# Seven-product matmuls in both MLPs' down projections and both attentions' output projections, with accumulator banks paired by use

## The chip, the cores and the metric

One core of a Trainium2 chip runs the whole program. The metric is the device time of one execution in microseconds. An execution's own time is the span from its first to its last instruction and a little more around it (1.75 us in the profiled one). The engines are TensorE (PE, with its weight loads listed apart as PEld), VectorE (DVE), ScalarE (ACT), GpSimd (POOL) and SyncE (SP). SP issues the transfers of the weights; POOL issues most other transfers.

## What is computed

Two decoder layers on 256 tokens of width 2048, all in fp32. Each layer is a token mixer, a cross-attention to 256 memory rows, and an MLP with a squared ReLU. Layer 0 mixes by a gMLP, layer 1 by an S5 state-space layer.

```python
def memory_attention(h, mem_n, w_q, w_kv, w_o):
    ...
    p = jax.nn.softmax(scores, axis=-1).astype(v.dtype)
    o = jnp.einsum('bhsm,bmhd->bshd', p, v).reshape(bsz, seq, X_HEADS * X_HEAD_DIM)
    return o @ w_o

def squared_relu_mlp(h, w_up, w_down):
    return jnp.square(jax.nn.relu(h @ w_up)) @ w_down
```

`w_o` is 2048 x 2048, `w_up` 2048 x 8192 and `w_down` 8192 x 2048. The change concerns the two products `o @ w_o` and `(...) @ w_down`, in both layers.

## The kernel before

**Precision.** An fp32 product is made of three products of rounded parts: hi x hi, hi x lo and lo x hi. Activations are kept as such pairs. Each weight tile (two row blocks of 128, 512 columns: 128x1024 numbers, 512 KB) is loaded by SP into `wraw` (`wload`, 4 buffers); ACT casts it to `whi` (L101), and DVE subtracts to get `wlo` (L102); `whi` and `wlo` have 3 buffers each. This pair of instructions is called a split below. A tile then feeds 12 matmuls of 128x512: 2 row blocks, 2 halves of the tokens, 3 products. Every weight tile ends with a `tick`.

**A down or output product.** The output is taken in four column blocks `n` of 512. For each, 8 weight tiles are added up in one accumulator (`psA`: 2 accumulators of two banks, one bank for each half of the tokens), and DVE gathers the result into the residual `x`. `w_o` goes through `gemm_tok` (gather at L527), layer 0's `w_down` through `gemm_hid` (matmuls L700 to L702, gather L560). The MLP runs in four quarters of the hidden width: an up stage (`gemm_feat`, 32 tiles of `f_w_up`), then a down stage (4 column blocks, 32 tiles of `f_w_down`).

**The seven-product form.** Layer 1's down products go through `gemm_seven` (seven calls of it; the last two column blocks of the last quarter are done otherwise). A call makes two column blocks at once. Of each block's 8 weight tiles the first two (token halves x row tiles x column blocks: 2 x 2 x 2 blocks) are multiplied in Strassen's manner by 7 block products of 6 matmuls each, instead of 8. The other 12 tiles are direct. The block products need sums of token blocks (`token_sums`, once for each quarter: four operations of 128x256 and one split) and sums of raw weight tiles (L653, L663, L669, L674: 128x1024 each). The raw tiles are fetched into `ws`. Some block results belong to two outputs, so ACT copies them out of the bank (`keep`, L646), and DVE gathers the copies.

**What sets the order.** The program is scheduled when it is built: each engine then runs its instructions in that fixed order and waits in place. SP's loads too are one queue in order. `self.side` holds work that is put between the ticks. In layer 0's MLP this is the preparation of the S5 layer's matrices (`ssm_prep`, L911 to L962): 109 pieces, one every two ticks, each with small operations on DVE, some on PE and ACT, and POOL transfers (`bcq` in, `Qd`, `Kd` and `Pd` out). S5 reads those back as `pq`, `dq` and `qq` (L986). `self.at` puts work a given number of ticks ahead: `nxt.chunk(x, n)` makes column block `n` of the next stage's normalized, transposed activations, with PE transposes (L214). The activations live in the `act` pool, 2 buffers of 128 x 16 x 512 numbers: `hT`, the input of the stage, and in the attention `oT`. Between attention 0 and layer 0's MLP `regroup` (L1235) writes `x` to DRAM and reads it back in another order of rows, 2 MB out and 2 MB in, on POOL's queue.

Of the kernel before, what the change touches and what calls it, by code (L numbers as in the profile page):

```python
# [21 lines left out]
NCH = D // NB  # L22
# [16 lines left out]
class Trunk:  # L39
# [395 lines left out]
    def attention(self, x, layer, cur, nxt):  # L435
# [3 lines left out]
        with tc.tile_pool(name="at", bufs=2, reuse_waits="tile") as ap:  # L439
# [59 lines left out]
            for hd in range(HEADS):  # L499
# [3 lines left out]
                for t in range(2):  # L503
# [19 lines left out]
            nxt.start()  # L523
            for j in range(NCH):
                acc = self.gemm_tok(oT, wo, j)
                xc = x[:, :, j * NB:(j + 1) * NB]
                nc.vector.tensor_tensor(out=xc, in0=acc, in1=xc, op=ALU.add)  # L527
                self.at(1, lambda j=j: nxt.chunk(x, j))


    def mlp(self, x, layer, cur, nxt):
# [3 lines left out]
        with tc.tile_pool(name="ml", bufs=4, reuse_waits="tile") as mp:  # L535
            r2 = mp.tile([P, 32 if layer else 56], F32, name="r2", bufs=1)[:, 0:2]
            for b in range(DFF // D):
                hid = []
                for n in range(NCH):
# [3 lines left out]
                    for i in range(2):  # L543
                        r = mp.tile([P, 2, S], F32, name="r", bufs=2)
# [32 lines left out]

    def token_sums(self, pool, a1, a2):


        v = self.nc.vector
        s = pool.tile([P, 4, 2, P], F32, name="s", tag="ws", bufs=4)
        a11, a21, a12, a22 = (a[:, :, t * P:(t + 1) * P] for a in (a1, a2) for t in range(2))
# [3 lines left out]
        v.tensor_tensor(out=s[:, 3], in0=a12, in1=s[:, 1], op=ALU.subtract)  # L587
        sh = pool.tile([P, 4, 2, P], F32R, name="sh", bufs=1)
        sl = pool.tile([P, 4, 2, P], F32R, name="sl", bufs=1)
        self.split(sh, sl, s)  # L590
        return sh, sl

    def gemm_seven(self, pool, hid, sums, w, n0, k0, gather):

# [39 lines left out]

        plain = {j: list(range(2, KT // KB)) for j in range(2)}

        def direct(j):
            kc = plain[j].pop(0)
            hi, lo = self.wtile(w, n0 + j, kc0 + kc)
            for t in (1, 0):  # L640
                into((t, j), range(KB), lambda kk: token(KB * kc + kk, t), hi, lo, not plain[j])
            self.tick()

        def keep(key):
            t = pool.tile([P, NB], F32, name="kept", bufs=4)
            nc.scalar.copy(out=t, in_=banks[key])  # L646
# [5 lines left out]
        run = pool.tile([P, KB * NB], F32, name="run", bufs=1)  # L652
# [4 lines left out]
        acc0 = self.psA.tile([P, 2, NB], F32, name="acc")  # L657
        banks.update({(t, 0): acc0[:, t, :] for t in range(2)})
# [18 lines left out]
        v.tensor_tensor(out=u3, in0=u3, in1=m5, op=ALU.add)
# [659 lines left out]
```

## Time and profile before

| | |
|---|---|
| Median of 3 runs | 2847.34 us (2844.35 to 2847.85) |
| Profiled execution, its own time | 2847.75 us |
| Its span | 2846.0 us |
| Mean granted TensorE clock | 0.998 |
| HBM read, written | 553.88 MB, 22.94 MB |
| Weight queue (hardware) | 511.77 MB, 58.7% of 16 engines |
| POOL's queue (software) | 65.19 MB, 8.5% |

The stages that matter here, in us from the span's start: attention 0 ends near 674; layer 0's MLP follows until 1424, with down stages at 766 to 858, 954 to 1046, 1144 to 1236 and 1332 to 1424; then S5, attention 1, and layer 1's MLP at the end. Busy times of engines are sums of the records' durations. An idle engine is given with the instruction that released it. The records of PE overlap, so PE's pace is read from the starts.

### The profile page before, as it was taken

The numbers are of one execution on the slowest core, as the hardware profiler recorded it, in microseconds if no ns is written. First come the engines' busy times: TensorE is split into PE (matmuls) and PEld (weight loads), VectorE is DVE, ScalarE is ACT, GpSimd is POOL, SyncE is SP. The second block draws the span as 40 slices with busy tenths as digits, with TensorE's granted clock in tenths as the row PEclk, the third lists the DMA queues.
The fourth block names the chain that finished last, engine by engine and source line by source line (L and its number), as shares of the span: only waits on it lengthen the run. The fifth ranks groups of instructions, "written<-read, shape, count | busy, mean of one in ns | idle before, by whom it ended". The sixth has DMA issues, their size and how long they took to land.

```text
span 2846.0 us, 39638 instructions
## 1 busy us (share of the span) xinstructions
PE 2806.7 (99%) x15196; PEld 2350.1 (83%) x15196; DVE 1913.3 (67%) x2645; ACT 1373.7 (48%) x1767; POOL 204.7 (7%) x380
## 2 busy tenths in 40 slices
PE   8999999999999999999999999999999999999998
PEld 6888888888888888888777788888888888888886
DVE  6765655585778888787577666555556766667665
ACT  5445544444544444444455445444454545445453
POOL 1000000000022222222011000000000000000000
PEclk9999999999999999999999999999999999999999
DMA  8766665567677777777879776565566566565755
GB/s 287 216 208 200 193 181 176 169 178 238 187 221 220 221 220 214 220 224 207 234 243 297 215 211 206 170 182 179 178 185 216 168 215 184 171 215 163 221 156 156
DMA packets 180463, 579.56 MB, mean 204 GB/s; under 512 B 37440, under 2 KB 39664, under 8 KB 179504
## 3 DMA queue, kind: packets, MB, share of 16 engines
q1 hardware_dynamic: 141440, 511.77, 58.7%
q0 software_dynamic: 38688, 65.19, 8.5%
q8 instruction: 119, 1.95, 0.3%
q14 instruction: 72, 0.59, 0.1%
q10 hardware_dynamic: 144, 0.07, 0.0%
HBM read 553.88 MB, written 22.94 MB: 203 GB/s over the span
## 4 chain that ended last, share of the span: by engine, by line
PE 90%; DMA 4%; DVE 3%; ACT 1%; issue 1%; POOL 0%; SPq 0%; DVEq 0%; ACTq 0%; POOLq 0%
PE acc L163 24%; PE acc L165 12%; PE acc L623 9%; PE acc L147 9%; PE acc L146 9%; PE acc L145 9%; PE acc L702 4%; PE acc L701 4%; PE acc L700 4%; DVE wlo L102 1%; PE ps L515 1%; PE ps L459 1%; DMA wraw<-in_f_w_down 1%; ACT whi L101 1%; PE ps L214 1%
## 5 line engine op out<-in xcount | busy, mean ns | idle before, releaser
L102 DVE TENSOR_TENSOR wlo<-wraw,whi 128x1024 fp32r<-128x1024 f32 x924 | 1128.9, 1223 | 721.0 <-ACT whi L101 717.7
L101 ACT CAST whi<-wraw 128x1024 fp32r<-128x1024 f32 x924 | 971.5, 1052 | 1176.5 <-PE acc L163 384.7
L163 PE MATMUL acc<-act,whi 128*128 128x512 f32 x3072 | 1083.6, 396 | 0.6 <-ACT whi L101 0.6
L165 PE MATMUL acc<-act,wlo 128*128 128x256 f32 x3072 | 864.9, 282 | 1.9 <-DVE wlo L102 1.9
L163 PEld LDWEIGHTS acc<-act,whi 128*128 128x128 f32 x3072 | 576.1, 188 | 134.4 <-issue 1.6
L165 PEld LDWEIGHTS acc<-act,wlo 128*128 128x128 f32 x3072 | 580.4, 189 | 6.8 <-DVE wlo L102 3.4
L145 PE MATMUL acc<-whi,act 128*128 128x512 f32 x1248 | 490.7, 393 | 9.5 <-ACT whi L101 8.0
L146 PE MATMUL acc<-wlo,act 128*128 128x512 f32 x1248 | 488.7, 392 | 3.9 <-DVE wlo L102 3.7
L147 PE MATMUL acc<-whi,act 128*128 128x512 f32 x1248 | 487.7, 391 | 0.3 <-DVE act L102 0.3
L145 PEld LDWEIGHTS acc<-whi,act 128*128 128x128 f32 x1248 | 235.2, 188 | 58.9 <-ACT whi L101 8.5
L146 PEld LDWEIGHTS acc<-wlo,act 128*128 128x128 f32 x1248 | 235.2, 188 | 53.5 <-DVE wlo L102 6.3
L147 PEld LDWEIGHTS acc<-whi,act 128*128 128x128 f32 x1248 | 235.3, 189 | 48.5 <-DVE act L102 0.7
L701 PE MATMUL acc<-wlo,hh 128*128 128x512 f32 x544 | 215.2, 396 | 1.2 <-DVE wlo L102 1.2
L700 PE MATMUL acc<-whi,hh 128*128 128x512 f32 x544 | 214.7, 395 | 0.0
L702 PE MATMUL acc<-whi,hl 128*128 128x512 f32 x544 | 214.4, 394 | 0.0
L623 PE MATMUL acc<-whi,hh 128*128 128x512 f32 x378 | 148.1, 392 | 3.4 <-ACT kept L646 2.7
L623 PE MATMUL acc<-wlo,hh 128*128 128x512 f32 x378 | 147.5, 390 | 0.6 <-DVE wlo L102 0.6
L623 PE MATMUL acc<-whi,hl 128*128 128x512 f32 x378 | 147.2, 389 | 0.0
L701 PEld LDWEIGHTS acc<-wlo,hh 128*128 128x128 f32 x544 | 102.2, 188 | 25.2 <-DVE wlo L102 2.5
L702 PEld LDWEIGHTS acc<-whi,hl 128*128 128x128 f32 x544 | 102.2, 188 | 22.7 <-issue 1.6
L700 PEld LDWEIGHTS acc<-whi,hh 128*128 128x128 f32 x544 | 102.2, 188 | 22.7 <-ACT whi L101 0.4
L623 PEld LDWEIGHTS acc<-whi,hh 128*128 128x128 f32 x378 | 70.9, 188 | 21.6 <-ACT kept L646 5.3
(315 smaller groups left out, 2286.3 us busy)
## 6 DMA issues: line engine op xcount, KB each, us to landing
wraw<-in_f_w_up SPq DMA_DIRECT2D x256, 512.0 KB, 4.2
wraw<-in_f_w_down SPq DMA_DIRECT2D x228, 512.0 KB, 4.2
wraw<-in_a_w_in SPq DMA_DIRECT2D x64, 512.0 KB, 4.4
wraw<-in_x_w_q SPq DMA_DIRECT2D x64, 512.0 KB, 3.7
wraw<-in_x_w_k SPq DMA_DIRECT2D x64, 512.0 KB, 3.7
wraw<-in_x_w_v SPq DMA_DIRECT2D x64, 512.0 KB, 3.6
wraw<-in_x_w_o SPq DMA_DIRECT2D x64, 512.0 KB, 3.7
wraw<-in_b_w_out SPq DMA_DIRECT2D x64, 512.0 KB, 4.4
```

The lines of the kernel that those rows point to most:

```text
L101: self.nc.scalar.copy(out=hi, in_=src)
L102: self.nc.vector.tensor_tensor(out=lo, in0=src, in1=hi.bitcast(F32), op=ALU.subtract)
L145: nc.tensor.matmul(out[t], ah[:, kt, sl], hi[:, kk, :], start=st, stop=False)
L146: nc.tensor.matmul(out[t], ah[:, kt, sl], lo[:, kk, :], start=False, stop=False)
L147: nc.tensor.matmul(out[t], al[:, kt, sl], hi[:, kk, :], start=False, stop=en)
L163: nc.tensor.matmul(acc[:, f, :], hi[:, kk, sl], both[:, kt].rearrange("p a s -> p (a s)"), start=st, stop=False, skip_group_check=True)
L165: nc.tensor.matmul(acc[:, f, 0:S], lo[:, kk, sl], ah[:, kt, :], start=False, stop=en, skip_group_check=True)
L214: nc.tensor.transpose(pt[:, kk, t * P:(t + 1) * P], src[:, t, c:c + P], self.ident)
L623: mm = lambda s, m, e: nc.tensor.matmul(out, s, m, start=key not in begun, stop=e, skip_group_check=True)
L700: nc.tensor.matmul(acc[:, t, :], ah[:, kt % 4, sl], hi[:, kk, :], start=st, stop=False)
L701: nc.tensor.matmul(acc[:, t, :], ah[:, kt % 4, sl], lo[:, kk, :], start=False, stop=False)
L702: nc.tensor.matmul(acc[:, t, :], al[:, kt % 4, sl], hi[:, kk, :], start=False, stop=en)
```

## The change

`gemm_seven` now also does layer 0's down products (two calls in each quarter, eight in all) and both output projections (two calls each). Twelve calls are new, and layer 1's MLP keeps its seven. Inside `gemm_seven` the two accumulators are now paired as they become free: `acc[0]` holds the outputs (1,0) and (0,1), `acc[1]` holds (0,0) and (1,1) (token half, column block). All four raw tiles are fetched at the start of a call. The last direct tiles of the two column blocks are interleaved, so that `acc[0]` is complete first, is gathered, and then `acc[1]`.

Room for the buffers: in the attentions, tags that the softmax no longer needs; in layer 0's MLP one tile `room` of 128 x 8 x 1024 numbers in the `act` pool, in the memory that `oT` of attention 0 had. The chunks of the next norm now come in twos behind each call.

```diff
@@ attention
+                if hd == 0:
+                    for fp in range(2):
+                        o = ap.tile([P, 2, S], F32, name="o", tag="e")
+                        nc.scalar.copy(out=o, in_=ops[fp])
+                        ops[fp] = o
+                    sums = self.token_sums(ap.tile([P, KB * NB], F32, name="s", tag="qh"),
+                                           lambda: ap.tile([P, 4, 2, P], F32R, name="sums", tag="kh"), *ops)
...
-            for j in range(NCH):
-                acc = self.gemm_tok(oT, wo, j)
-                xc = x[:, :, j * NB:(j + 1) * NB]
-                nc.vector.tensor_tensor(out=xc, in0=acc, in1=xc, op=ALU.add)
-                self.at(1, lambda j=j: nxt.chunk(x, j))
+            for j in range(0, NCH, 2):
+                self.gemm_seven((ws, run, kept), lambda kt, t: [f[:, kt, t * P:(t + 1) * P] for f in oT[:2]],
+                                sums, wo, j, 0, gather)
+                for n in (j, j + 1):
+                    self.at(1 + n - j, lambda n=n: nxt.chunk(x, n))
@@ mlp
+            else:
+                room = self.act.tile([P, 8, KB * NB], F32, name="room", tag="act")
+                count = [iter(range(200)) for _ in range(2)]
+                ws = lambda: room[:, next(count[0]) % 4]
+                sm = lambda: mp.tile([P, 4, 2, P], F32R, name="sums", bufs=2)
+                run = st = lambda: room[:, 4]
+                kept = lambda i: room[:, 5 + 2 * (i in (1, 2)), i // 3 * NB:(i // 3 + 1) * NB]
+                rt = lambda: room[:, 6].rearrange("p (i k s) -> p i k s", i=2, k=2)[:, next(count[1]) % 2]
...
-                    if nxt.closing and not (end and n >= NCH - 2):
+                    if not (nxt.closing and end and n >= NCH - 2):
@@ gemm_seven
-        acc1 = self.psA.tile([P, 2, NB], F32, name="acc")
-        banks = {(t, 1): acc1[:, t, :] for t in range(2)}
-        fetch(0, 0), fetch(0, 1)
+        acc = [self.psA.tile([P, 2, NB], F32, name="acc") for _ in range(2)]
+        banks = {(1, 0): acc[0][:, 0], (0, 1): acc[0][:, 1], (0, 0): acc[1][:, 0], (1, 1): acc[1][:, 1]}
+        for i, j in ((0, 0), (0, 1), (1, 0), (1, 1)):
+            fetch(i, j)
...
         summed((0, 1), 0, run, True)
-        m5 = keep((0, 1))
-        direct(1)
...
         block((1, 0), 0, 0, raw[0, 0], True)
-        m1 = keep((1, 0))
-        fetch(1, 1)
-        direct(1)
+        m5, m1 = keep((0, 1), 0), keep((1, 0), 1)
+        block((0, 0), 0, 1, raw[1, 0])
+        whole(1, 1)
...
-        for t in range(2):
-            gather(t, n0 + 1, banks[t, 1])
-        while plain[0]:
-            direct(0)
-        for t in range(2):
-            gather(t, n0, banks[t, 0])
+        while len(todo[0]) > 1 or len(todo[1]) > 1:
+            j = len(todo[1]) > len(todo[0])
+            whole(j, j)
+        ends = [direct(0, 1), direct(1, 0)]
+        for keys in (((1, 0), (0, 1)), ((0, 0), (1, 1))):
+            for e in ends:
+                next(e)
+            for t, j in keys:
+                gather(t, n0 + j, banks[t, j])
```

Lines move by 44 and less: in the changed kernel the gathers are L599 (MLP) and L546 (attention), the weight sums L698, L704, L709 and L714, the sum of kept parts L718, the fetch L646, the matmuls of `gemm_seven` L661; L948 has become L992, and L959 is L1003.

Three places of the order show what is moved. The first is SP's queue from the last `w_o` loads (`in_x_w_o`) over the start of layer 0's MLP, after the change; `room` are the raw tiles of its first seven-product call.

```order
L118 DMA wraw<-in_x_w_o 128x1024 x16
L118 DMA wraw<-in_f_w_up 128x1024 x5
L646 DMA room<-in_f_w_down 128x1024
L118 DMA wraw<-in_f_w_up 128x1024
L646 DMA room<-in_f_w_down 128x1024
L118 DMA wraw<-in_f_w_up 128x1024
L646 DMA room<-in_f_w_down 128x1024
L118 DMA wraw<-in_f_w_up 128x1024
L646 DMA room<-in_f_w_down 128x1024
L118 DMA wraw<-in_f_w_up 128x1024 x24
```

And before, at the same place:

```order
L118 DMA wraw<-in_x_w_v 128x1024 x32
L118 DMA wraw<-in_x_w_o 128x1024 x32
L118 DMA wraw<-in_f_w_up 128x1024 x32
L118 DMA wraw<-in_f_w_down 128x1024 x32
```

Four loads for the down stage have moved ahead of the up stage, and the first of them waits until PE has read `oT` for the last time.

The second place is DVE at the boundary between the two calls of layer 0's first down stage, after the change (`wlo<-room` is a split of a block product, `wlo<-wraw` of a direct tile, L599 a gather, L704 a weight sum; `tq`, `qt`, `kd`, `pq` are side work).

```order
L976 TENSOR_TENSOR tq<-T_5639,bcq 128x576
L102 TENSOR_TENSOR wlo<-room,whi 128x1024
L977 TENSOR_TENSOR qt<-qt,tq 128x4x9x16
L599 SCALAR_TENSOR_TENSOR x<-acc,r_5644,x 128x512 x2
L704 TENSOR_TENSOR room<-room 128x1024
L599 SCALAR_TENSOR_TENSOR x<-acc,r_5644,x 128x512 x2
L102 TENSOR_TENSOR wlo<-room,whi 128x1024 x2
L102 TENSOR_TENSOR wlo<-wraw,whi 128x1024
L992 SCALAR_TENSOR_TENSOR kd<-eye,dsk,ps 128x16
L599 SCALAR_TENSOR_TENSOR x<-room,r_5644,x 128x512
```

And before, at a boundary between two column blocks of that stage:

```order
L932 TENSOR_TENSOR tq<-T_5578,bb 128x4x128
L913 TENSOR_SCALAR bcq<-bcq,sg 128x128
L102 TENSOR_TENSOR wlo<-wraw,whi 128x1024 x2
L948 SCALAR_TENSOR_TENSOR kd<-eye,dsk,ps 128x16
L921 TENSOR_TENSOR bb<-F,bcq 128x4x16 x2
L931 TENSOR_TENSOR qt<-T_5577,bcq 128x4x9x16
L560 SCALAR_TENSOR_TENSOR x<-acc,r_5583,x 128x512 x2
L102 TENSOR_TENSOR wlo<-wraw,whi 128x1024 x2
```

Where two tiles were split ahead of two gathers, now one product's weights are split ahead of four gathers and a weight sum. At the later boundaries of this kind the second product's split stands between the two pairs of gathers.

The third place is PE at the end of the side work, after the change: its last four transposes (L1003). L145 to L147 are the matmuls of S5's first product; 57 of them stand ahead of these transposes.

```order
L145 MATMUL acc<-whi,act 128x512
L146 MATMUL acc<-wlo,act 128x512
L147 MATMUL acc<-whi,act 128x512
L1003 MATMUL ps<-ident,pq 128x128
L214 MATMUL ps<-ident,x 128x128 x4
L145 MATMUL acc<-whi,act 128x512
L1003 MATMUL ps<-ident,pq 128x128
L146 MATMUL acc<-wlo,act 128x512
L1003 MATMUL ps<-ident,pq 128x128
L147 MATMUL acc<-whi,act 128x512
L1003 MATMUL ps<-ident,pq 128x128
```

And before, where they stand among the matmuls of layer 0's last down stage:

```order
L700 MATMUL acc<-whi,hh 128x512
L959 MATMUL ps<-ident,pq 128x128
L701 MATMUL acc<-wlo,hh 128x512
L959 MATMUL ps<-ident,pq 128x128
L702 MATMUL acc<-whi,hl 128x512
L959 MATMUL ps<-ident,pq 128x128
L700 MATMUL acc<-whi,hh 128x512
L959 MATMUL ps<-ident,pq 128x128
```

The end of the side work has moved from the MLP into the next layer, since the MLP has 224 ticks instead of 256.

In all the program has 72 matmul rows of 128x512 fewer on PE, 36 splits more (973 to 1009 on DVE), 48 more weight sums, and the same number of transfers.

More of the change, by code (lines that the diff above doesn't have):

```diff
@@ L508, in attention @@
                 ph, pl = pTs[hd]
+                ops = [self.ps([P, 2, S]) for _ in range(2)]
                 for fp in range(2):
-                    op = self.ps([P, 2, S])
+                    op = ops[fp]
                     for k in range(2):
@@ L521, in attention, with kept, gather @@
                     self.split(oT[0][:, kt:kt + 2, :], oT[1][:, kt:kt + 2, :], op)
-            nxt.start()
-            for j in range(NCH):
-                acc = self.gemm_tok(oT, wo, j)
-                xc = x[:, :, j * NB:(j + 1) * NB]
-                nc.vector.tensor_tensor(out=xc, in0=acc, in1=xc, op=ALU.add)
-                self.at(1, lambda j=j: nxt.chunk(x, j))
+                if hd == 0:
[5 more added lines that the diff above has]
+                                           lambda: ap.tile([P, 4, 2, P], F32R, name="sums", tag="kh"), *ops)
+            nxt.start()
+            count = iter(range(100))
+            ws = lambda: ap.tile([P, KB * NB], F32, name="ws", tag=("ql", "qh")[next(count) % 2])
+            run = lambda: ap.tile([P, KB * NB], F32, name="run", tag="kl")
+            pair = {}
+            def kept(i):
+                if i in (1, 2):
+                    return ap.tile([P, NB], F32, name="kept", tag="z")
+                if i == 0:
+                    pair[0] = ap.tile([P, 2, NB], F32, name="kept2", tag="kl")
+                return pair[0][:, i // 3, :]
+            def gather(t, n, part):
+                xc = x[:, t, n * NB:(n + 1) * NB]
+                nc.vector.tensor_tensor(out=xc, in0=part, in1=xc, op=ALU.add)
+            for j in range(0, NCH, 2):
[3 more added lines that the diff above has]
+                    self.at(1 + n - j, lambda n=n: nxt.chunk(x, n))
     def mlp(self, x, layer, cur, nxt):
@@ L549, in mlp @@
                     hid.append((h, l))
-                    if nxt.closing and n == 0:
-                        sums = self.token_sums(mp, *rs)
+                    if n == 0:
+                        sums = self.token_sums(st(), sm, *rs)
                 if b == 0:
@@ L564, in mlp @@
                     end = b == DFF // D - 1
-                    if nxt.closing and not (end and n >= NCH - 2):
+                    if not (nxt.closing and end and n >= NCH - 2):
                         if n % 2 == 0:
-                            self.gemm_seven(mp, hid, sums, wd, n, b * KT, gather)
+                            self.gemm_seven((ws, run, kept), lambda kt, t: [f[:, kt % 4, t * P:(t + 1) * P]
+                                                                            for f in hid[kt // 4]],
+                                            sums, wd, n, b * KT, gather)
                     elif nxt.closing and end and n == NCH - 1:
@@ L587, in token_sums, with gemm_seven @@
         v.tensor_tensor(out=s[:, 3], in0=a12, in1=s[:, 1], op=ALU.subtract)
-        sh = pool.tile([P, 4, 2, P], F32R, name="sh", bufs=1)
-        sl = pool.tile([P, 4, 2, P], F32R, name="sl", bufs=1)
+        sh, sl = tile(), tile()
         self.split(sh, sl, s)
         return sh, sl
-    def gemm_seven(self, pool, hid, sums, w, n0, k0, gather):
+    def gemm_seven(self, tiles, token, sums, w, n0, k0, gather):
         nc = self.nc
@@ L600, in gemm_seven @@
         kc0 = k0 // KB
+        ws, run, kept = tiles
         raw, half = {}, lambda t: t.rearrange("p (k c) -> p k c", k=KB)
         def fetch(i, j):
-            t = pool.tile([P, KB * NB], F32, name="ws", bufs=4)
+            t = ws()
             self.fed = nc.sync.dma_start(out=half(t), in_=w[n0 + j, kc0 + i]).ins
@@ L626, in into @@
                 mm(ah, lo[:, kk, :], False)
-                mm(al, hi[:, kk, :], end and kk == KB - 1)
+                mm(al, hi[:, kk, :], True)
         def block(key, t, i, src, end=False):
@@ L633, in summed, with direct @@
             into(key, range(KB), lambda kk: [f[:, k, kk, :] for f in sums], *parts(src), end)
-        plain = {j: list(range(2, KT // KB)) for j in range(2)}
-        def direct(j):
-            kc = plain[j].pop(0)
+        todo = {j: list(range(2, KT // KB)) for j in range(2)}
+        def direct(j, first):
+            kc = todo[j].pop(0)
             hi, lo = self.wtile(w, n0 + j, kc0 + kc)
-            for t in (1, 0):
-                into((t, j), range(KB), lambda kk: token(KB * kc + kk, t), hi, lo, not plain[j])
+            for t in (first, 1 - first):
+                into((t, j), range(KB), lambda kk: token(KB * kc + kk, t), hi, lo)
+                yield
@@ L642, in direct, with whole, keep @@
             self.tick()
-        def keep(key):
-            t = pool.tile([P, NB], F32, name="kept", bufs=4)
+        def whole(*a):
+            for _ in direct(*a):
+                pass
+        def keep(key, i):
+            t = kept(i)
             nc.scalar.copy(out=t, in_=banks[key])
             return t
-        acc1 = self.psA.tile([P, 2, NB], F32, name="acc")
-        banks = {(t, 1): acc1[:, t, :] for t in range(2)}
-        fetch(0, 0), fetch(0, 1)
-        run = pool.tile([P, KB * NB], F32, name="run", bufs=1)
+        acc = [self.psA.tile([P, 2, NB], F32, name="acc") for _ in range(2)]
@@ L684, in gemm_seven @@
-        while plain[0]:
-            direct(0)
-        for t in range(2):
-            gather(t, n0, banks[t, 0])
+        while len(todo[0]) > 1 or len(todo[1]) > 1:
[7 more added lines that the diff above has]
+                gather(t, n0 + j, banks[t, j])
+        for e in ends:
+            next(e, None)
```

34 lines of the change are left out of this document (18 added, 16 removed).

## The prediction

> **What bounds the kernel now.** I read the page first (busy shares, then the chain that ended last), then the whole list of what PE waits for, then busy time by stage.
>
> ```profile
> span 2846.0 us, 39638 instructions
> PE 2806.7 (99%) x15196; PEld 2350.1 (83%) x15196; DVE 1913.3 (67%) x2645; ACT 1373.7 (48%) x1767; POOL 204.7 (7%) x380
> ...
> PE 90%; DMA 4%; DVE 3%; ACT 1%; issue 1%; POOL 0%; SPq 0%; DVEq 0%; ACTq 0%; POOLq 0%
> ```
> PE is busy 99% of the span and is 90% of the chain: a matmul removed shortens the kernel, unless something else then comes late. The rows of PE's waits that touch this change are short:
>
> ```profile
> PE acc L623 <- ACT kept L646: 2.7, 4, 0.7
> ...
> PE acc L623 <- DVE x L560: 0.7, 3, 0.2
> PE acc L623 <- DVE wlo L102: 0.6, 2, 0.4
> ```
> These 4.0 us are all that the seven calls in layer 1 lose now. The pace of PE is read from starts, because its records overlap:
>
> ```profile
> 2018.48 0.39 PE L145 MATMUL acc<-whi,act 128*128 128x512 f32 x1
> 2018.71 0.39 PE L146 MATMUL acc<-wlo,act 128*128 128x512 f32 x1
> 2018.94 0.39 PE L147 MATMUL acc<-whi,act 128*128 128x512 f32 x1
> ```
> One 128x512 matmul per 0.227 us; a direct weight tile (12) takes 2.72, a product (6) 1.36. Now the stages: a down stage of layer 0, the up stage behind it, the two at the first hand-over, and the end of the V stage of attention 0 (columns: window, length, busy of PE, PEld, DVE, ACT, POOL, clock, DMA share, GB/s).
>
> ```profile
> 609.30:632.00 22.70, 22.70 (x105) 18.85 (x104) 22.36 (x60) 9.94 (x12) 0.00 (x0) 1.00 0.64 185
> 672.00:700.00 28.00, 28.00 (x164) 24.40 (x163) 14.54 (x16) 10.98 (x14) 4.99 (x10) 1.00 0.98 278
> 700.00:728.00 28.00, 26.61 (x151) 22.63 (x150) 21.50 (x43) 19.94 (x34) 0.00 (x0) 1.00 0.74 225
> 766.00:858.40 92.40, 92.40 (x443) 74.38 (x442) 71.24 (x116) 39.85 (x48) 18.38 (x32) 1.00 0.73 214
> 858.40:954.00 95.60, 95.60 (x584) 81.67 (x583) 83.23 (x138) 44.52 (x58) 26.52 (x48) 1.00 0.73 219
> ```
> In layer 0's MLP, DVE is already at 77 and 87%, since the S5 preparation runs beside it, and PE is never idle there. At 672 to 700 DMA is full.
>
> **The change part by part.**
>
> *1. Matmuls.* Each of twelve new calls does 186 matmuls instead of 192: 8 calls in layer 0's MLP, 4 in the attentions. 72 x 0.227 = **-16.3 us**. This is certain; the other terms say how much is given back.
>
> *2. DVE in layer 0's MLP.* Prices:
>
> ```profile
> L102 DVE TENSOR_TENSOR wlo<-wraw,whi 128x1024 fp32r<-128x1024 f32 x924 | 1128.9, 1223 | 721.0 <-ACT whi L101 717.7
> L677 DVE TENSOR_TENSOR kept<-kept 128x512 f32<-128x512 f32 x7 | 4.8, 686 | 0.0
> L584 DVE TENSOR_TENSOR s<-r 128x256 f32<-128x256 f32 x4 | 1.7, 424 | 0.1
> ...
> 2234.64 2.36 DVE L102 TENSOR_TENSOR wlo<-ws,whi 128x1024 fp32r<-128x1024 f32 x2
> ...
> 858.92 1.40 DVE L560 SCALAR_TENSOR_TENSOR x<-acc,r,x 128x512 f32<-128x512 f32 x2
> ```
> Back to back, a 128x1024 operation costs 1.14 us (2.36 for two, less the overlap) and a gather 0.66. A down stage gets 6 more splits (38 for 32) and 8 weight sums, 14 x 1.14 = 16.0; 6 more gathers, 4.0; two additions of kept parts, 1.2: +21.2. It has 24 ticks instead of 32, so 12 side pieces instead of 16. A piece is (71.2 - 32 x 1.14 - 6 gathers at 0.66 - some 2 of the last hidden group) / 16 = 1.8 us, so -7.2. DVE comes to 85.2, PE to 92.4 - 12 x 0.227 - some 2 for four pieces' small matmuls = 87.7. The token sums (4 x 0.42 + 1.14 = 2.8) fall into the up stage: 86 of 95.6, which hides them. But in the down stage DVE also waits, in order:
>
> ```profile
> L931 DVE TENSOR_TENSOR pq<-T,bb 128x512 f32<-128x512 f32 x5 | 3.4, 689 | 1.1 <-PE ps L959 1.1
> L921 DVE TENSOR_TENSOR bb<-F,bcq 128x64 f32<-128x64 f32 x8 | 1.4, 221 | 1.8 <-PE ps L943 1.8
> L913 DVE TENSOR_SCALAR bcq<-bcq,sg 128x128 f32<-128x128 f32 x5 | 1.4, 285 | 4.2 <-DMA bcq<-in_b_bc 4.2
> ```
> That is 7.1 per down stage. 85.2 + 7.1 = 92.3 is 4.6 over PE's 87.7. If none of the waits shrinks, four stages lose 18; if DVE, being later, finds its data ready, nothing. The call boundary has a price of its own: the last two direct tiles and the next first product hold all three buffers of whi and wlo, so the second product's split stands beside gathers that wait for PE's last matmuls. Where it stands behind both pairs (the DVE rows of the order above), it is ready 1.33 + 1.14 us after PE's end, and PE, with one product ahead, needs it at 1.36 + 0.23: 0.9 lost. Where it stands between the pairs, the third product's split is some 0.4 late. 8 boundaries x 0.5 = 4, and 2 for the waits: **+6** (0 to +22).
>
> *3. Loads at the start of layer 0's MLP.* Four fetches of `room`, 2.1 MB, stand on SP behind `f_w_up` loads 5, 6, 7 and 8, and go out as soon as PE has read `oT` for the last time. At that place now:
>
> ```profile
> 692.43 1.05 ACT L101 CAST whi<-wraw 128x1024 fp32r<-128x1024 f32 x1 [1.78 <-PE acc L163]
> 700.47 1.05 ACT L101 CAST whi<-wraw 128x1024 fp32r<-128x1024 f32 x1 [6.99 <-DMA wraw<-in_f_w_up]
> ...
> 673.37 1.08 POOL L1240 DMA_DIRECT2D xd<-x  x2 [178.38 <-DVE x L527]
> 683.54 3.92 POOL L1245 DMA_DIRECT2D x<-xd  x8 [9.09 <-DMA xd<-x]
> ...
> 680.00:684.00 4.00, 4.00 (x24) 3.48 (x24) 1.83 (x2) 1.15 (x2) 0.46 (x1) 1.00 0.96 348
> ...
> 701.57 0.49 PE L163 MATMUL acc<-act,whi 128*128 128x512 f32 x1 [0.63 <-ACT whi L101]
> 702.83 0.39 PE L165 MATMUL acc<-act,wlo 128*128 128x256 f32 x1 [0.77 <-DVE wlo L102]
> ```
> Counted by the casts, the tile that ACT waits 6.99 us for is the tenth: due 2.8 us after the ninth's cast at 692.43, it is 5.2 late. The regroup has taken the bandwidth; PE uses up its lead and loses 1.4. All four fetches stand ahead of that tile, and no lead is left to hide them: 2.1 MB at the 278 GB/s of the window are 7.5 us, at the 348 of its best stretch 6.0. I take **+6** (0, if the regroup yields and not the weights, to +11 at the lower share that it leaves them).
>
> *4. Attentions.* Their DVE has no side work; the first call's sums and splits meet the V stage's end, where DVE was 98.5% busy and PE lost nothing. Four boundaries at 0.4, and the last two chunks of the next norm now both behind the last call: **+2** (0 to +6).
>
> *5. Layer 1's MLP.* The 4.0 us above go, since a kept copy no longer blocks a direct tile in the same accumulator; the boundary takes 7 x 0.4 back: **-1.5** (-4 to +3).
>
> *6. Side work runs into S5.* 109 pieces, one every two ticks, end at tick 218: of 256 before, of 224 now. Before, the last write of `Pd` and the first fetches behind it lay far ahead of their use:
>
> ```profile
> 1348.34 0.57 POOL L962 DMA_DIRECT2D Pd<-po  x1 [5.67 <-ACT po L961]
> 1348.89 2.14 POOL L986 DMA_DIRECT2D pq<-Pd  x4
> ...
> 1423.83 0.39 PE L700 MATMUL acc<-whi,hh 128*128 128x512 f32 x1
> ...
> 1462.15 1.96 PE L1040 MATMUL ps<-pq,us 128*32 128x128 f32 x64
> ...
> 1360.00:1395.00 35.00, 31.93 (x139) 24.84 (x138) 16.73 (x21) 15.05 (x21) 0.00 (x0) 1.00 0.92 214
> 1425.00:1445.00 20.00, 20.00 (x94) 16.60 (x93) 13.57 (x28) 10.24 (x16) 3.42 (x8) 1.00 0.94 311
> ```
> Now the last side transposes stand 57 matmuls (12.9 us) into S5's first product (the PE rows of the order), and `pq` is used 38 us after that product's start. The 25 us between must hold a write and 2 MB of `pq`, at the 311 - 188 (one 0.512 MB tile per 2.72 us) = 123 GB/s that the weights leave: 17 us, just enough. `dq` and `qq`, 4 MB more, then press on the weights, while the crowding at 1360 to 1395 (3.1 us of idle PE) goes in part: **+1.5** (-3 to +8).
>
> **Sum.** Against the profiled execution, 2847.75 us (0.4 above the median of 2847.34): -16.3 + 6 + 6 + 2 - 1.5 + 1.5 = -2.3, so **2845.5**. About 0.2%, 5.7 us, is what a measurement here can tell from no change: faster is below 2841.6, slower above 2853.0.
>
> **The rivals.**
>
> *A, the cover holds.* The window at 609 shows DVE 98.5% busy for 23 us with PE at 22.70 of 22.70, so a crowded DVE need not stop PE; and if the regroup yields, the room loads are free. Then terms 2 and 3 are nothing: -16.3 + 2 - 1.5 = 2832 with term 6 at nothing. Against it: the 6.99 us wait is a DMA's.
>
> *B, slower: DVE sets layer 0's MLP.* Its waits for `bcq` come from a loop through POOL (issue, load, DVE, next issue) and don't shrink when DVE is late. Each down stage then takes 92.3 instead of 87.7: +18 in place of +6, so 2857.5. It decides from where DVE busy plus its waits for data passes PE's time in a down window, 87.7 us; the up stages, at 90%, can't prepare more than three tiles ahead.
>
> *C, slower: the POOL queue starves.* If dense DVE work delays POOL's own transfers, the `bcq` wait grows.
>
> ```profile
> DVE bcq L913 <- DMA bcq<-in_b_bc: 28.3, 14, 5.4
> ...
> 794.75 2.30 POOL L951 DMA_DIRECT2D Kd<-kd  x4 [9.02 <-issue]
> ```
> 28.3 us in three quarters are 38 in four; half as much again is +19: 2864.5. Against it: four issues took 2.30 us beside a DVE at 77%, and 2.14 at 1348.89 in a thinner stretch. [...]
>
> *D, S5 starts hungry.* Term 6 at its upper end, 2845.5 + 6.5 = 2852.
>
> That the change doesn't remove the matmuls is excluded: the order of PE has 72 rows of 128x512 less.
>
> **How the numbers follow.** Forecast 0.50 (2840 to 2854), A 0.27, B 0.15, C 0.04, D 0.04. The likeliest gives 2845.5. The forecast's own spread puts 0.05 under 2841.6 and 0.04 over 2853.0; with A below, B and C above, and half of D above: faster 0.32, same 0.43, slower 0.25. The range 2832 to 2860 leaves out half of A (0.12 or so below) and the far part of B and C.
>
> **What would show it.** Step 1: 72 fewer PE records, and down windows of layer 0 shorter than 92.4. Step 2: PE waits for wlo between 766 and 1400, four at the ends of first calls; if DVE's `bcq` waits fall below 28.3, A is near, if they grow, B or C. Step 3: an idle PE near 700 to 712, released by `f_w_up`, of about 7 us instead of 1.4. Step 5: no wait on a kept copy in layer 1. Step 6: L1040 of the first S5 group waiting for `pq`. I am wrong if PE's waits in layer 0's MLP stay under 3 us in all (then 2836 or less), or if they pass 20.

## The result and the profile after

The changed kernel takes 2859.15 us (median of 6 runs, 2858.09 to 2865.64), the kernel before beside it 2847.6: a ratio of 1.0045, 95% interval 1.0034 to 1.0056. It is slower by 0.45%. The forecast was 2845.5, no change. The page of the changed kernel, with span, busy times and chain:

```profile
span 2856.4 us, 39731 instructions
...
PE 2802.8 (98%) x15124; PEld 2343.0 (82%) x15124; DVE 2041.8 (71%) x2815; ACT 1438.3 (50%) x1861; POOL 204.0 (7%) x380
...
PE 82%; DVE 7%; DMA 5%; issue 3%; ACT 2%; POOL 1%; SPq 0%; DVEq 0%; ACTq 0%; POOLq 0%
```

PE has 72 matmuls less, as forecast, and yet the span is 10.4 us longer: PE is idle for 53.6 us instead of 39.3, and its busy time fell by 3.9 us only, where 72 matmuls at 0.227 us are 16.3: the other matmuls took longer. DVE has 128 us more to do. What PE waits for in the changed kernel (us in total, times, longest):

```profile
PE acc L661 <- DVE wlo L102: 12.9, 6, 4.5
...
PE ps L1070 <- ACT u L1059: 6.5, 3, 4.5
...
PE acc L165 <- DVE wlo L102: 3.2, 5, 0.8
PE acc L163 <- ACT whi L101: 2.0, 2, 1.6
...
PE acc L661 <- DVE x L599: 0.5, 2, 0.3
```

The wait on a kept copy is gone from the list. New are three long waits on `wlo` in layer 0's down stages (3.9, 2.9 and 4.5 us) and one of 4.5 at the start of S5. Stage by stage, each counted from its first large matmul to that of the next:

| Stage | before, us | after, us | difference |
|---|---|---|---|
| up to the end of attention 0's K stage | 479.37 | 478.76 | -0.6 |
| attention 0, V and output | 192.28 | 189.37 | -2.9 |
| layer 0's MLP: up 1 | 94.33 | 100.99 | +6.7 |
| down 1, up 2 | 188.1 | 186.8 | -1.3 |
| down 2 | 92.14 | 97.36 | +5.2 |
| up 3 | 97.70 | 95.86 | -1.8 |
| down 3 | 92.09 | 96.03 | +3.9 |
| up 4, down 4 | 191.5 | 187.7 | -3.8 |
| S5 | 314.40 | 324.23 | +9.8 |
| attention 1, Q and K | 191.5 | 192.2 | +0.8 |
| attention 1, V and output | 192.31 | 188.98 | -3.3 |
| layer 1's MLP | 720.38 | 718.12 | -2.3 |

Four stages lose most. Their rows of the windows before (length, busy of PE, PEld, DVE, ACT, POOL, clock, DMA share, GB/s):

```profile
671.65:765.98 94.33, 92.94 (x532) 80.38 (x531) 60.26 (x92) 48.70 (x69) 4.99 (x10) 1.00 0.75 224
...
954.07:1046.21 92.14, 92.14 (x443) 73.86 (x442) 71.19 (x111) 38.04 (x44) 19.93 (x37) 1.00 0.73 221
...
1143.91:1236.00 92.09, 92.09 (x441) 74.13 (x437) 70.97 (x110) 38.26 (x44) 22.13 (x40) 1.00 0.74 217
...
1427.45:1741.85 314.40, 307.48 (x2304) 247.86 (x2303) 204.04 (x343) 162.16 (x253) 28.06 (x53) 1.00 0.80 238
```

And after:

```profile
668.13:769.12 100.99, 95.83 (x539) 82.41 (x539) 82.75 (x177) 50.76 (x74) 5.00 (x10) 0.98 0.75 228
...
955.93:1053.29 97.36, 90.58 (x417) 72.60 (x413) 81.52 (x118) 47.30 (x56) 17.67 (x32) 0.98 0.68 208
...
1149.15:1245.18 96.03, 91.39 (x419) 72.14 (x418) 81.30 (x117) 47.16 (x56) 17.77 (x33) 0.98 0.69 210
...
1432.85:1757.08 324.23, 313.79 (x2325) 252.28 (x2323) 206.83 (x349) 165.92 (x263) 35.65 (x67) 0.98 0.84 245
```

All four have a clock of 0.98, where before it was 1.00. The timeline of the changed kernel at down 2 shows what happens: first POOL, then DVE, then PE.

```profile
991.23 0.54 POOL L956 DMA_DIRECT2D bcq<-in_b_bc  x1 [4.08 <-DVE tq L976]
...
992.76 0.69 DVE L976 TENSOR_TENSOR tq<-T,bb 128x512 f32<-128x512 f32 x1
998.76 0.29 DVE L957 TENSOR_SCALAR bcq<-bcq,sg 128x128 f32<-128x128 f32 x1 [5.31 <-DMA bcq<-in_b_bc]
998.96 1.22 DVE L102 TENSOR_TENSOR wlo<-wraw,whi 128x1024 fp32r<-128x1024 f32 x1
...
1000.23 0.79 PE L661 MATMUL acc<-wlo,hh 128*128 128x512 f32 x1 [3.86 <-DVE wlo L102]
1000.83 0.63 PE L661 MATMUL acc<-whi,hl 128*128 128x512 f32 x1
1001.25 0.63 PE L661 MATMUL acc<-whi,hh 128*128 128x512 f32 x1
...
1003.69 0.40 PE L661 MATMUL acc<-whi,hh 128*128 128x512 f32 x1
1003.93 0.40 PE L661 MATMUL acc<-wlo,hh 128*128 128x512 f32 x1
```

DVE waits 5.3 us for a load of side work (`bcq`); the split that PE needs stands behind it in DVE's fixed order; PE uses up its lead and stands still for 3.9 us. And then it runs slowly: 0.42 us from one matmul to the next until some 3.4 us later, then 0.24 and less again; the granted clock is 0.51 from 1000.2 to 1003.6 and 1.00 behind that. Half speed for 3.4 us costs another 1.7. The other two long waits have the same in front of them: 5.3 us for `bcq` at the end of down 2 (2.9 us of PE), 7.3 in down 3 (4.5). DVE's two largest waits over layer 0's MLP from down 1 on, before and after (the one for `bcq` before is 28.3 us in 14, longest 5.4):

```profile
DVE wlo L102 <- ACT whi L101: 96.9, 76, 4.6
...
DVE bcq L957 <- DMA bcq<-in_b_bc: 30.8, 10, 7.3
DVE wlo L102 <- ACT whi L101: 25.8, 30, 2.4
```

A DVE that waits for ACT's casts is ahead of its work: this slack has shrunk from 96.9 us to 25.8. At the start of S5 (POOL, PE, and behind the dots the weight load from the chain):

```profile
1448.12 0.57 POOL L1006 DMA_DIRECT2D Pd<-po  x1 [6.10 <-ACT po L1005]
1448.68 2.14 POOL L1030 DMA_DIRECT2D pq<-Pd  x4
1450.78 1.87 POOL L1030 DMA_DIRECT2D dq<-Kd  x3
...
1472.88 1.97 PE L1070 MATMUL ps<-ident,u 128*128 128x128 f32 x8 [4.54 <-ACT u L1059]
...
1457.61 12.81 DMA wraw<-in_b_w_in
```

The last side write is at 1448.12, 15 us into S5 (before: 79 us ahead of it), and the fetches of `pq` and `dq` come straight behind it. A weight tile then takes 12.8 us, where PE uses one every 2.72. Of the 9.8 us that S5 loses, 3.5 are idle PE (10.4 us against 6.9); the other 6.3 are longer busy time of PE, with the slow stretches (granted clock 0.50 from 1471.2 to 1478.0 and from 1536.0 to 1539.4) and 21 small matmuls more.

### The profile page after: what moved, and what is told of

Same layout as the page of the kernel before. It is cut to its first block, busy times and chain, and to the rows that moved or that the text cites. A ratio compares the mean times of both kernels' runs of the same rounds, so it can differ in the third digit from the quotient of the medians.

```text
span 2856.4 us, 39731 instructions
## 1 busy us (share of the span) xinstructions
PE 2802.8 (98%) x15124; PEld 2343.0 (82%) x15124; DVE 2041.8 (71%) x2815; ACT 1438.3 (50%) x1861; POOL 204.0 (7%) x380
## 4 chain that ended last, share of the span: by engine, by line
PE 82%; DVE 7%; DMA 5%; issue 3%; ACT 2%; POOL 1%; SPq 0%; DVEq 0%; ACTq 0%; POOLq 0%
PE acc L661 22%; PE acc L163 22%; PE acc L165 11%; PE acc L146 7%; PE acc L147 7%; PE acc L145 7%; DVE wlo L102 3%; DMA bcq<-in_b_bc 2%; DMA wraw<-in_f_w_up 1%; ACT whi L101 1%; PE ps L516 1%; PE ps L459 1%; DMA Kd<-kd 1%; PE ps L214 1%; DMA wraw<-in_a_w_in 1%
## 5 line engine op out<-in xcount | busy, mean ns | idle before, releaser
L102 DVE TENSOR_TENSOR wlo<-wraw,whi 128x1024 fp32r<-128x1024 f32 x876 | 1069.7, 1223 | 608.0 <-ACT whi L101 603.9
L101 ACT CAST whi<-wraw 128x1024 fp32r<-128x1024 f32 x876 | 921.2, 1052 | 1015.4 <-PE acc L163 356.8
L145 PE MATMUL acc<-whi,act 128*128 128x512 f32 x992 | 391.1, 394 | 8.5 <-ACT whi L101 7.0
L146 PE MATMUL acc<-wlo,act 128*128 128x512 f32 x992 | 389.5, 393 | 4.6 <-DVE wlo L102 4.6
L147 PE MATMUL acc<-whi,act 128*128 128x512 f32 x992 | 388.5, 392 | 0.3 <-DVE act L102 0.3
L661 PE MATMUL acc<-wlo,hh 128*128 128x512 f32 x810 | 319.9, 395 | 12.9 <-DVE wlo L102 12.9
L661 PE MATMUL acc<-whi,hh 128*128 128x512 f32 x810 | 318.9, 394 | 1.0 <-DVE x L599 0.2
L661 PE MATMUL acc<-whi,hl 128*128 128x512 f32 x810 | 318.3, 393 | 0.0
L145 PEld LDWEIGHTS acc<-whi,act 128*128 128x128 f32 x992 | 187.0, 189 | 48.9 <-ACT whi L101 8.4
L146 PEld LDWEIGHTS acc<-wlo,act 128*128 128x128 f32 x992 | 187.2, 189 | 44.6 <-DVE wlo L102 7.1
L147 PEld LDWEIGHTS acc<-whi,act 128*128 128x128 f32 x992 | 187.3, 189 | 38.7 <-DVE act L102 0.7
L661 PEld LDWEIGHTS acc<-wlo,hh 128*128 128x128 f32 x810 | 152.9, 189 | 48.7 <-DVE wlo L102 16.1
L661 PEld LDWEIGHTS acc<-whi,hh 128*128 128x128 f32 x810 | 152.7, 189 | 37.0 <-DVE r L169 2.2
L661 PEld LDWEIGHTS acc<-whi,hl 128*128 128x128 f32 x810 | 153.0, 189 | 32.2 <-issue 0.4
L661 PE MATMUL acc<-whi,act 128*128 128x512 f32 x432 | 135.8, 390 | 0.0
L661 PE MATMUL acc<-whi,sums 128*128 128x512 f32 x304 | 107.1, 393 | 0.3 <-DVE x L599 0.3
L661 PEld LDWEIGHTS acc<-whi,act 128*128 128x128 f32 x432 | 80.8, 188 | 16.6
L101 ACT CAST whi<-room 128x1024 fp32r<-128x1024 f32 x56 | 59.1, 1055 | 65.5 <-PE acc L661 45.4
```

Of the source, the lines that this page charges most:

```text
L101: self.nc.scalar.copy(out=hi, in_=src)
L102: self.nc.vector.tensor_tensor(out=lo, in0=src, in1=hi.bitcast(F32), op=ALU.subtract)
L145: nc.tensor.matmul(out[t], ah[:, kt, sl], hi[:, kk, :], start=st, stop=False)
L146: nc.tensor.matmul(out[t], ah[:, kt, sl], lo[:, kk, :], start=False, stop=False)
L147: nc.tensor.matmul(out[t], al[:, kt, sl], hi[:, kk, :], start=False, stop=en)
L661: mm = lambda s, m, e: nc.tensor.matmul(out, s, m, start=key not in begun, stop=e, skip_group_check=True)
```

## The experiments

Theory 1: transfers that come late at three places (room loads, `bcq`, S5's first fetches), each made longer by the halved clock. Theory 2: DVE in layer 0's MLP simply has too much to do.

**Side work at the old pace.** In each call two more side pieces, behind the second and fourth sum product:

```diff
         def summed(key, k, src, end=False):
...
+            if k % 2 and self.side and self.every == 2:
+                with self.later(self.lag):
+                    self.side.pop(0)()
```

> Layer 0's down stages take 16 side pieces again instead of 12 (two more per call, behind the second and the fourth sum product), so that the side work ends inside the MLP, as before. Theory 1 (late transfers at three places: the S5 fetches, the room loads, the bcq loads, each made longer by a halved clock behind it): the S5 stage, 324.5 us in the changed kernel and 314.6 before, falls to 314 to 317, and the time by 5 to 10, to 2850 to 2854. Theory 2 (DVE in layer 0's MLP is simply too full, wherever the loads stand): the down stages lose what S5 gains, 2858 or more.

Measured: 2888.18 us, ratio 1.0136 (1.0119 to 1.0153). S5 did fall, to 317.2 us, and its wait on `u` from 6.5 to 2.9 us; but the down stages paid far more. Windows of the down stages 1 to 3 and of S5:

```profile
770.67:862.55 91.88, 90.60 (x427) 71.69 (x426) 84.67 (x133) 48.81 (x61) 18.43 (x32) 1.00 0.70 219
961.32:1061.10 99.78, 91.46 (x424) 70.97 (x422) 86.55 (x128) 48.84 (x58) 21.32 (x39) 0.99 0.67 206
1163.01:1265.86 102.85, 95.75 (x429) 75.84 (x426) 86.58 (x132) 47.82 (x58) 22.21 (x40) 0.93 0.67 204
1471.74:1788.95 317.21, 309.85 (x2312) 249.92 (x2311) 206.66 (x348) 164.68 (x261) 28.15 (x53) 0.99 0.79 236
```

So an earlier end of the side work helps S5, and the side work in the down stages costs too. On the latter theory 2 gains.

**Room loads later.** `hold` is the sixteenth `f_w_up` load:

```diff
+            if self.hold:
+                with self.tc.issue_after(self.hold):
+                    self.fed = load()
```

> The first four fetches of room are ordered on SP behind the sixteenth f_w_up load of the up stage, and not behind the fifth. Theory 1: the first up stage of layer 0's MLP falls from 101.0 us to 94 to 96 (94.3 before), the time by 4 to 6, to 2853 to 2855. Theory 2: PE meets the same full DVE a little earlier, and later stages give it back: 2857 to 2860.

Measured: 2853.72 us, ratio 1.0028 (1.0019 to 1.0038), 5.4 us less than the changed kernel. The first up stage is as short as before, at full clock:

```profile
668.43:762.65 94.22, 92.96 (x540) 81.11 (x540) 82.86 (x177) 50.95 (x74) 5.01 (x10) 1.00 0.77 244
```

The room loads cost what the stage table shows, 6.7 us. Not all of it stays won: down 3 is 98.2 us here, 2.2 more than in the changed kernel.

**Layer 0's MLP plain.** The condition is again `nxt.closing and not (end and n >= NCH - 2)`, and layer 0 has its own `r` buffers.

> Layer 0's MLP goes back to the plain product with its own buffers; both attentions and layer 1's MLP keep the changed form. Theories 1 and 2 alike: the S5 stage and layer 0's MLP are as before, the attentions keep -6 (2 x (192.3 to 189.4 and 189.0)), layer 1's MLP -2.3: 2838 to 2841. A third theory (the form brings nothing wherever it is put, since a stall follows each call): 2846 or more.

Measured: 2840.17 us, ratio 0.9972 (0.9963 to 0.9982). Run once more beside another kernel:

> The same program as e3_layer0_plain, once more, for the comparison beside it: 2839 to 2842.

2842.64 us, ratio 0.9982 (0.9973 to 0.9991), a little above what was expected. Attentions and layer 1's MLP gain; all of the loss lies in layer 0's MLP and what it does to S5. The third theory is out.

**bcq loaded earlier.** At each quad the load of the quad after next:

```diff
-            bcq = pool.tile([P, 4, 4, 16], F32, name="bcq", bufs=3)
-            nc.gpsimd.dma_start(out=bcq, in_=a["b_bc"][q])
+            for r in ((0, 1, 2) if q == 0 else (q + 2,)):
+                if r < G // 4:
+                    early[r] = pool.tile([P, 4, 4, 16], F32, name="bcq", bufs=3)
+                    nc.gpsimd.dma_start(out=early[r], in_=a["b_bc"][r])
+            bcq = early.pop(q)
```

> The bcq load of a quad is issued two quads ahead in the program, in the same three buffers; nothing else changes. Theory 1: DVE's waits for bcq in layer 0's MLP, 30.8 us in 10, fall under 15; PE's two stalls of 3.9 and 4.5 us behind them go with the halved clock that follows each (1.7 each): the down stages of 97.4 and 96.0 fall to 90 to 92, the time to 2848 to 2852. Theory 2: the wait moves to another operation of DVE and PE stalls as long: 2856 to 2860.

Measured: 2860.22 us, ratio 1.0043 (1.0028 to 1.0058), and the wait itself did not change (DVE's waits, 766 to 1430):

```profile
DVE bcq L962 <- DMA bcq<-in_b_bc: 30.3, 11, 7.2
```

The reason is the buffers. In both kernels POOL issues the load as soon as DVE has read the buffer's old content for the last time (`tq` at 990.16 and the issue at 991.23 in the changed kernel, 993.33 and 994.40 here), and in both the next use of the buffer stands four instructions behind that `tq` in DVE's order. So the edit moved nothing, and this run says nothing on theory 1: it did not take the cause away. A fourth buffer was not tried.

**Fewer side pieces.** `tr.lag, tr.every = 200, 3`:

> The changed kernel with one side piece every three ticks instead of two: 8 pieces in a down stage of layer 0, not 12 (and 16 in the run before this); what is left of the side work is done in one go ahead of S5, which pays for it. Theory 2 (the side work and the block products together fill DVE in the down stages): second and third down stage, 97.4 and 96.0 us with 12 pieces and 99.8 and 102.9 with 16, come down to 88 to 91; no clock window at half speed between 720 and 1420; S5 gets longer, and the time is 2855 to 2885. Theory 1 (single late bcq loads, whatever DVE's load): one or two stalls of 3 us and more stay, 94 to 97.

Measured: 2945.23 us, ratio 1.0344 (1.0327 to 1.0360), 60 us above the expected range, since a third of the side work is left for the end, where the clock falls too (mean 0.979). Down stages 1 to 3:

```profile
771.82:858.11 86.29, 86.29 (x391) 70.70 (x389) 71.35 (x94) 46.52 (x55) 2.82 (x4) 1.00 0.65 208
951.50:1038.56 87.06, 87.06 (x406) 70.71 (x405) 73.32 (x95) 46.42 (x53) 12.67 (x23) 1.00 0.70 221
1133.53:1221.75 88.22, 88.22 (x411) 71.14 (x409) 76.29 (x103) 46.91 (x54) 13.27 (x24) 1.00 0.70 220
```

With 8, 12 and 16 pieces the second down stage takes 87.1, 97.4 and 99.8 us, the third 88.2, 96.0 and 102.9. That is what theory 2 said. But DVE is busy for only 81.5 of the 97.4 us: its work alone does not fill the stage. And with 8 pieces no wait for `bcq` in these three stages is longer than 2.0 us, so this run does not tell the work from the waits.

**Some of DVE's side work on GpSimd.** Room loads late, and `times(...)` of `quad_p` with `nc.gpsimd`:

> The changed kernel with the room loads behind the sixteenth f_w_up load, and with the three 128x512 operations of each quad's P matrices done by GpSimd instead of VectorE. Theory 2: DVE has 2.1 us less to do for each quad, the down stages two and three fall from 97.5 and 98.2 to 90 to 93, and the time from 2853.7 to 2840 to 2847. Theory 1: as DVE waits for transfers and not for work, nothing or little: 2850 to 2856. A third possibility: GpSimd is slower at them and its queue holds up the bcq, Kd and Qd transfers behind: 2856 or more.

Measured: 2921.46 us, ratio 1.0259 (1.0239 to 1.0278). The third possibility, and more of it: DVE now waits for GpSimd, which takes 1.6 us for an operation that takes DVE 0.69.

```profile
DVE tq L975 <- POOL pq L986: 58.1, 16, 11.1
DVE bcq L966 <- DMA bcq<-in_b_bc: 40.3, 18, 7.2
```

**Side work late, without block products.** Layer 0's MLP plain, and ahead of the side work 16 empty pieces:

```diff
+        tr.side += [lambda: None] * 16
         tr.ssm_prep(pp)
```

> Layer 0's MLP plain (as in the run of 2840 us), but its side work begins 32 ticks later, so that it ends 6 ticks before the MLP does, as in the changed kernel. No block product in that MLP. If the late end of the side work is what costs S5 its 10 us, the S5 stage rises from 315.2 to 322 to 326 us and the time to 2847 to 2851. If S5 loses them for another reason (the norm's chunks in pairs, DVE behind after the MLP), it stays at 315 and the time at 2840.

Measured: 2845.06 us, ratio 0.9989 (0.9979 to 0.9998), and in S5:

```profile
1425.37:1746.02 320.65, 312.49 (x2320) 251.20 (x2319) 206.25 (x349) 164.14 (x260) 36.22 (x68) 0.99 0.82 248
```

320.7 us where the same kernel with its side work early has 314.9: 5.7 of the 9.8 us come without any block product in that MLP. The effect is there, but smaller than expected, although the last write of `Pd` is later here (19 us into S5, not 15).

**The pairing alone.** The kernel before with only layer 1's seven calls in the new form:

> The kernel before with one part of the change: the seven calls of layer 1's MLP in the new form (banks paired by use, fetches at the start, ends interleaved); attentions and layer 0's MLP plain. By the trace of the changed kernel, layer 1's MLP is 2.3 us shorter: 2844.5 to 2846.5. If that came from something else, 2847 to 2849.

Measured: 2845.12 us, ratio 0.9992 (0.9982 to 1.0002). The time is as expected, but the interval reaches 1, so the gain is not told from none by the times alone.

**Block products in layer 0's last quarter only.** For layer 0 the condition is `end`, with `hold` set in that quarter:

> Both attentions and layer 1's MLP in the changed form, and of layer 0's MLP the last quarter alone, with its first room fetches behind the sixteenth f_w_up load of that quarter. In the plain kernel the side work is nearly over there (DVE 50 of 95.8 us busy in that down stage), and with 8 ticks fewer in all it still ends inside the MLP. If the side work on DVE and its late end are what spoils the form in layer 0, it pays here: the stage loses 12 matmuls, 2.7 us, and some of its 3.1 us of stalls, S5 stays at 315: 2836 to 2838.5. If the form itself disturbs layer 0 (the room in the activation pool, pairs of chunks), 2840 or more.

Measured: 2847.3 us, ratio 0.9996 (0.9987 to 1.0004), 4.7 above the plain one beside it. The last down stage takes 101.4 us, not 94.1. The chain of waits there:

```profile
1348.50 11.34 DMA room<-in_f_w_down
...
1362.25 14.03 DMA wraw<-in_f_w_down
```

By the time the form itself would be to blame (2840 or more). The trace says otherwise: here S5's fetches (`pq` from 1345) meet the loads of the raw tiles, one more place where transfers crowd: 11.3 us for a raw tile and 14.0 for a weight tile in that chain. S5 itself stayed at 316.

**No bcq transfer.** The first three quads' `bcq` serve all 32:

```diff
+            if q < 3:
+                kept.append(pool.tile([P, 4, 4, 16], F32, name="bcq", bufs=3))
+                nc.gpsimd.dma_start(out=kept[q], in_=a["b_bc"][q])
+            bcq = kept[q % 3]
```

> The changed kernel, which loads bcq for the first three quads only and uses these three again for the other 29 (their own B and C matrices are left out): the same operations on DVE and PE, but no transfer to wait for. If PE's stalls of 3.9 and 4.5 us come from single waits for bcq that DVE's lead no longer covers, they go with the half-speed windows behind them: down stages two and three from 97.4 and 96.0 to 88 to 91, the time to 2845 to 2850. If it is DVE's work alone, 95 or more, and 2855 to 2860.

Measured: 2843.26 us, ratio 0.9981 (0.9972 to 0.9990). Down 2, down 3 and S5:

```profile
955.47:1044.17 88.70, 88.70 (x416) 71.65 (x413) 81.01 (x117) 47.34 (x56) 15.42 (x28) 1.00 0.71 223
1140.03:1229.36 89.33, 89.33 (x420) 71.22 (x418) 80.54 (x116) 47.23 (x56) 15.51 (x28) 1.00 0.71 221
1416.44:1741.15 324.71, 311.94 (x2324) 250.74 (x2323) 206.82 (x349) 165.93 (x263) 35.63 (x67) 0.99 0.84 244
```

DVE is as busy as in the changed kernel (81.0 and 80.5 us), and in these two stages PE is never idle. This settles it: what the down stages lose is the wait for `bcq`, not the work. S5 is untouched by it.

**bcq on ACT's queue, and the three together.** Room loads late and `nc.scalar.dma_start` for `bcq`:

> All of the computation; the room loads behind the sixteenth f_w_up load, and bcq issued from ACT's queue, past Kd, Qd and Pd on POOL's. If the waits for bcq come from its place on POOL's queue, they fall under 10 us in all, the down stages go to 89 to 92, and with the room loads' 5 us the time is 2840 to 2846 (S5 keeps its 324). If ACT's casts now wait for the buffers of bcq, or the transfer itself is slow beside the weights, 2850 or more.

Measured: 2843.05 us, ratio 0.9978 (0.9969 to 0.9988). DVE's waits for `bcq` are 12.5 us in 5, where the kernel with late room loads alone has 27.6 in 10. Not quite under 10: a wait of 4.6 us is left in down 2 and stops PE for 2.9. Down 2 and S5:

```profile
951.42:1044.71 93.29, 90.39 (x416) 72.54 (x413) 80.87 (x118) 47.38 (x56) 15.45 (x28) 0.98 0.69 215
1417.36:1741.64 324.28, 313.77 (x2325) 252.31 (x2323) 206.78 (x349) 166.21 (x263) 35.64 (x67) 0.98 0.83 245
```

Then one side piece more in each call:

> As h2_bcq_act, with one side piece more in each call (14 in a down stage), so that the side work ends some 15 ticks before the MLP does. S5 falls from 324 to 315 to 318. If DVE, without waits for bcq, can carry 14 pieces, the down stages stay at 90 to 93 and the time is 2833 to 2840; if 14 are too many by themselves, stages of 95 and more, and 2848 or more.

Measured: 2843.3 us, ratio 0.9982 (0.9973 to 0.9991). Down 1 to 3 and S5:

```profile
764.32:854.84 90.52, 89.72 (x418) 71.77 (x417) 83.77 (x129) 48.51 (x60) 13.32 (x23) 1.00 0.69 220
950.79:1042.64 91.85, 90.61 (x423) 71.70 (x422) 83.27 (x121) 47.89 (x56) 16.44 (x30) 1.00 0.71 222
1138.58:1232.92 94.34, 92.24 (x423) 72.82 (x421) 83.33 (x121) 47.89 (x56) 16.24 (x29) 0.98 0.70 219
1424.65:1739.93 315.28, 308.51 (x2313) 248.72 (x2311) 206.60 (x348) 164.78 (x261) 28.01 (x53) 1.00 0.79 238
```

S5 falls from 324.3 to 315.3 by the earlier end of the side work alone, block products and all. But with 14 pieces a wait of 4.5 us for `bcq` stops PE once more in down 3, for 2.1 us; from down 1 to down 4 the MLP is longer by what S5 gains (660.3 us against 651.4), and the time is above the 2833 to 2840 expected. Both versions beat the kernel before and the changed one; the simpler one, with layer 0's MLP plain, is as fast within the intervals.

## Why the forecast was wrong, point by point

1. **Matmuls, -16.3.** Right: 15196 records became 15124.
2. **DVE in layer 0's MLP, +6.** This step failed by size. From down 1 to down 4 the stages come to +2.3 us, where 48 matmuls less are -10.9: the price was 13.2. The prediction had the right operations (85.2 us of DVE work in a down stage; 83.5 measured in the first), named the wait for `bcq`, and then took 2 of its 18 us, on the ground that "if DVE, being later, finds its data ready, nothing" is lost. The data was not ready: the waits come to 30.8 us against 28.3 before, in 10 instead of 14, so each is longer.

   Above all, long ones now stand in down stages: before, none there was above 1.8 us. The cover is thinner too: before, the one long wait, 5.4 us in an up stage, left PE running for 6.0 us and cost it 1.2; now two of 5.3 left it 2.9 and 3.9 us and cost 3.9 and 2.9, and one of 7.3 left it 5.7 and cost 4.5. That a busier DVE has built up less lead fits its shrunken slack, but no run shows it by itself.

   The three stalls are 11.3 us; half speed behind two of them (3.4 us each) is some 3.4 more, and a little came back elsewhere. The 13.2 has the 3.1 us of idle PE that went in down 4 taken off already; the prediction counts them in its term for S5. Counted like that, this step is 16.3 and S5 6.7.

   Rival B, with its 18, was nearer. Its reason (a loop through POOL) is borne out in part: the load waits for DVE's last use of the buffer, and past POOL's queue the waits are less than half. But it had four stages lose alike, where three stalls in two stages make up most, and its total of 2857.5 is so near the measured time partly by luck, since it left S5 at +1.5. Rival C's 38 us for four quarters is a wrong reading: before, there is no wait for `bcq` after 1331, and 28.3 is the whole.

   The boundaries, put at 4, cost 0.5 us on gathers and nothing else that the waits show: of the 12.9 us at L661, 11.3 are these three, and 1.6 lie in layer 1.
3. **Room loads, +6.** Right: +6.7, and gone when the loads come later.
4. **Attentions, +2.** Too dear: the two stages are 2.9 and 3.3 shorter where 12 matmuls each are 2.7. Nothing was given back.
5. **Layer 1's MLP, -1.5.** About right: -2.3.
6. **S5, +1.5.** This step failed most: +9.8, above even its upper end of 8. The place was right, and the late end of the side work as the cause (one side piece more in each call gives 9.0 back). The mechanism was not: the sum asked whether `pq` arrives in time ("17 us, just enough") and let `dq` and `qq`, which "press on the weights", cost next to nothing; it is a weight tile that came late, and PE never waits for `pq`. S5's start was also read 3 us too early: its first matmul is at 1427, not 1424, so that 22 us remained and not 25. The idle time at 1360 to 1395 did go, as hoped: in down 4 PE is idle for 3.1 us before and never after. (The stage is 3.4 us shorter; its 12 matmuls less are 2.7, and it now carries side work to its end.)
7. **What no term had: the clock.** The forecast counted a stall at its length. The mean clock fell from 0.998 to 0.995; 0.003 of 2856 us is about 9 us, in the four stages that lose. Behind the stall of 3.9 us the granted clock was 0.51 for 3.4 us, from 1000.2 on. A stall of 1.82 us in the changed kernel's S5 was followed by such a stretch as well, 0.50 from 1536.0 to 1539.4; behind one of 1.81 in the kernel before, at 1520, the clock stayed at 1.00. What decides it was not shown.

The terms as measured, -16.3 + 13.2 + 6.7 + 9.8, and the small ones (-0.8 in the attentions beside their matmuls, -2.3 in layer 1's MLP, +0.2 elsewhere) give +10.5; the spans differ by 10.4. One thing is open: why the late side work costs S5 9.8 us behind block products and 5.7 behind plain ones.

## What to carry to other kernels

Ask of a change that fills an engine not only whether its busy time still fits, but which waits stand in its fixed order and how much lead covers them: a wait of 5 us that cost 1 behind a DVE with slack cost 3 to 4 behind a fuller one, in another kind of stage. Side work that is paced by a count of steps moves when the steps become fewer, and its end, with the transfers that follow it, may land in the next stage. Price a stall of the matmul engine above its length where the clock falls behind it: here it fell to 0.51 for 3.4 us, some 1.7 us of work, behind two of the three stalls in the down stages.

## What the runs showed of the hardware

In the changed kernel stalls of PE of 1.8, 3.9, 4.5 and 4.5 us, and two of 1.6 and 0.8 close together, came with a granted clock of 0.50 for some 3.4 us, in which 128x512 matmuls started every 0.42 us instead of 0.23; at S5's start it was 6.8 us, from 1471.2, still in the stall, to 1478.0. Behind the stall of 1.8 us the stretch began 1.5 us after PE had started again. Behind stalls of 1.5, 1.7 and 2.9 us (PE's starts at 1567, 1503 and 1049) the clock stayed at 1.00; in the run with `bcq` on ACT's queue, down 2 with its stall of 2.9 had a mean clock of 0.98. GpSimd took 1.2 to 1.6 us for an fp32 operation of 128x512 between tiles, DVE 0.69. A load of 128 KB on POOL's queue, issued behind other side transfers while the weights streamed, took 7.5 us to its use at 991 and 11.6 at 1217; moved to ACT's queue, with the room loads late in both, it made DVE wait 12.5 us in all instead of 27.6.
